# A two-layer hybrid trunk: mLSTM's causal mask by a selection on GpSimd, both chunks' decays in a step of their own, the gates' step first, and another order of the first loads

## The chip, the cores and the metric

One core of one Trainium2 chip runs the whole program. The metric is the device time of one execution in microseconds (us). A kernel's time is the median of its runs; lower is better.

## The reference, cut to what matters

Two layers over 1024 rows of 1024 features, all in float32. Each layer does this:

```
h = RMSNorm(x);  y = h @ W_in + b_in            # one projection for three groups
m_out = mLSTM(conv+SiLU(q), conv+SiLU(k), v, i, f)   # 4 heads x 64, chunkwise
h_out = HGRN2(...);  s_out = sliding window attention(...)
x = x + concat(m_out, h_out, s_out) @ W_out
x = x + relu(RMSNorm(x) @ W_up)^2 @ W_down      # 4096 wide
x = x + sigmoid(RMSNorm(x) @ W_g) * RMSNorm(p @ W_p)
```

The part that the change touches is the weight inside a chunk of mLSTM. With b the running sum of the log forget gates, i the input gates and m the stabiliser:

```
dmat    = where(causal, b_t - b_s + i_s, -inf)
w_intra = exp(dmat - m_t)                        # zero above the diagonal
s       = (q k^T) * w_intra
num     = s v + w_inter * (q C);   den likewise
```

So the weights of positions s later than t must come out as zero.

## The kernel before

**Dense work.** The rows are cut into two blocks of 512 (b = 0, 1). `gemm` works a product in slabs: one slab is two 128-row pieces of weights, loaded as `raw` on SyncE's queue, split into a rounded part `whi` (ScalarE, L395) and the remainder `wlo` (VectorE, L399), and used by 24 matmuls (4 output tiles x 2 pieces x 3 products) at L435 or L437. `gemm` yields after each slab. For layer 0 the `wlo` of block 0 is stored to memory by GpSimd's queue (L402) and loaded again for block 1 by the same queue (L397), into a ring of 4 buffers. In all VectorE splits 800 pieces.

**Mixers.** The three groups (`SWA`, `HGRN`, `MLSTM`) are generators of small steps, two of each for every (layer, block), one for each half block (hb) of 256 rows. `Emitter.run` emits one dense step, then as many mixer steps as a rate says, in turn among up to three active mixers. Counted with the last, empty one, `SWA` has 9 steps, `HGRN` 14 and `MLSTM` 9, so that a (layer, block) has 2 x 32 = 64. An `MLP` has 66 dense steps (2 of the norm, 8 x 4 of the up products, 16 x 2 of the down products). With `RATE_MLP` = 0.9 that makes 59 mixer steps; `PLE` goes on at 0.9. The mixers of block 1 of layer 0 are emitted in `MLP` and `PLE` of block 0 alone; those of layer 1 get 9 steps more in the projection before. Block 0 of layer 0 is mixed into the projection of block 1, at 2.5 steps to a slab. A scheduler then orders each engine's queue by emission, priority and what is ready; every engine works its queue in order.

**One MLSTM** (L1178 to L1302) covers two chunks of 128 rows. Its steps before the change: (1) convolution (L1192, L1194); (2) SiLU of q and k, copies into `qbd`, then the gates: transposes `pg` (L1209), the log sigmoid of 4 x 256 values (L354 to L357), two scans (L1217, L1218) and the rows `R` (a constant tile `G4`, L1220 to L1224) and their bfloat16 parts `Gb` (L1228 to L1231); (3) transposes `pt` of `R` (L1236), the decays between chunks (L1238), `cS`, `ee`, `dcy`; then for each chunk c two steps: (4, 6) the decays `pw` in a bank of PSUM, their exponentials `W` (L1259, 4 of 128x128), the scores `pS` (L1262) and the product `Pt` (L1265); (5, 7) the values and the state; (8) the output. The bank `pw` is begun by a matmul of an identity with a mask of 0 and -1e30 (L1253), on which four matmuls add the decays (L1255):

```
nc.tensor.matmul(pw3, self.identb, self.mmask.unsqueeze(1).broadcast_to([P, 4, P]), start=True, stop=False)
for h in range(4):
    nc.tensor.matmul(pw3[:, h, :], self.selb[:, h:h + 1].broadcast_to([P, P]), Gb[:, c * P:(c + 1) * P], start=False, stop=(h == 3))
```

The mixers, the norms' transposes (L498) and the transposes of `PLE` (L794) share 4 banks of PSUM (`mbank`).

**The opening.** `first_constants` emits WARM = 15 matmuls on a constant tile (L221) ahead of everything else. `load_x` asks for the first halves of 4 tiles of x, t = 0 and 2 on SyncE's queue, t = 1 and 3 on ScalarE's, and for the first two `raw` of the projection `skv` on SyncE's; then for the second halves. `first` interleaves the norm of block 0 (generator a) with the projection's slabs (generator c): a, c, c, a, then the rest of a (constants, mean square, its inverse root, transposes L574), then the rest of c.

Of the kernel before, what the change touches and what calls it, by code (L numbers as in the profile page):

```python
# [21 lines left out]
P = 128  # L22
# [16 lines left out]
RATE_IN00 = 1.9  # L39
RATE_IN01 = 2.5  # L40
RATE_IN = 0.7
RATE_MLP = 0.9
RATE_PLE = 0.9

ROOM = tuple(22 - 4 * max(0, (n + 2) // 4) + 2 for n in range(24)) + (8,)
# [111 lines left out]
class Trunk:  # L157
# [65 lines left out]
    def constants(self, rows):  # L223

        nc, io, cst = self.nc, self.io, self.cst
        L, S = self.L, self.S
        ap = nc.gpsimd
        nt = S // P
        ident = self.ident
        self.rs = [cst([P, 136], f"rows{l}") for l in range(L)]  # L230
        self.fb = cst([4, L], "fb")
        self.identb = cst([P, P], "identb", BF16)
        nc.vector.tensor_copy(self.identb, ident)
        mm = self.mmask = cst([P, P], "mmask", BF16)
        ap.memset(mm, 0.0)
        ap.affine_select(mm, mm, pattern=[[1, P]], compare_op=ALU.is_ge, fill=NEG, base=0, channel_multiplier=-1)
        am = self.amask = cst([P, 256], "amask", BF16)
        ap.memset(am, 0.0)
        ap.affine_select(am, am, pattern=[[1, 256]], compare_op=ALU.is_ge, fill=NEG, base=-1, channel_multiplier=-1)
        ap.affine_select(am, am, pattern=[[-1, 256]], compare_op=ALU.is_ge, fill=NEG, base=P, channel_multiplier=1)  # L240
        rm = self.rmask = cst([P, 512], "rmask", BF16)
        ap.memset(rm, 1.0)
        ap.memset(rm.rearrange("p (c t) -> p c t", t=P)[:, :, 0:1], 0.0)
        self.lmask = {}
        for w in (16, 8, 4, 2, 1):
            t = cst([P, 64], f"lm{w}", U8)
            ap.memset(t, 1)
            v = t.bitcast(I8)
            ap.affine_select(v, v, pattern=[[-2 * w, 64 // w], [0, w]], compare_op=ALU.is_ge, fill=0.0, base=0, channel_multiplier=1)
            ap.affine_select(v, v, pattern=[[2 * w, 64 // w], [0, w]], compare_op=ALU.is_ge, fill=0.0, base=w - 1, channel_multiplier=-1)  # L250
            self.lmask[w] = t
        self.selp = cst([P, 2, P], "selp")
        ap.memset(self.selp, 0.0)
        ap.memset(self.selp[64:68], 1.0)
        ap.affine_select(self.selp[64:68], self.selp[64:68], pattern=[[2, 2], [1, 2], [0, 64]], compare_op=ALU.is_equal, fill=0.0, base=0, channel_multiplier=-1)
        self.hind = cst([P, 2], "hind")
        ap.memset(self.hind, 0.0)
        ap.memset(self.hind[0:64, 0:1], 1.0)
        ap.memset(self.hind[64:128, 1:2], 1.0)

        self.qbd = cst([P, 2, 2, 256], "qbd")
        ap.memset(self.qbd, 0.0)
        self.hqb = []
        for i in range(2):
            t = cst([P, 2, 2, 2, 64], f"hqb{i}")
            ap.memset(t, 0.0)
            self.hqb.append(t)
        self.hqi = 0
        self.G4 = cst([P, 256], "G4")
        ap.memset(self.G4, 0.0)  # L270

        self.Gb = cst([P, 256], "Gb", BF16)
        ap.memset(self.Gb, 0.0)
        self.selb = cst([P, 4], "selb", BF16)
        ap.memset(self.selb, 0.0)
        for j in range(3):
            v = self.selb[32 * j:32 * j + 4]
            ap.memset(v, 1.0)
            end = ap.affine_select(v, v, pattern=[[-1, 4]], compare_op=ALU.is_equal, fill=0.0, base=0, channel_multiplier=1)
        with self.tc.issue_after(end.ins):  # L280
            for l in range(L):
                ap.dma_start(self.rs[l], io["rowS"][l:l + 1].broadcast_to([P, 136]))
            ap.dma_start(self.fb, io["fb"])
            rows(ap)
        self.cbd = cst([P, 2, 2, 65], "cbd")
        self.sbd = cst([P, 2, 2, 64], "sbd")
        self.ml = cst([4, 1], "ml")
        self.K = [[cst([P, 4, P], f"K{a}{b}", F32R) for b in range(2)] for a in range(2)]
        self.V = cst([P, 4, P], "V")
        self.kv_once = set()  # L290
# [229 lines left out]
    def load_x(self, b, src, first=False):  # L520
        X = [[None, None] for _ in range(4)]
        for h in range(2):
            for t in range(4):
                s = X[t][h] = self.get()
                eng = self.nc.gpsimd if not first else self.nc.scalar if (h, t % 2) == (0, 1) else self.nc.sync
                with self.tc.high_priority(2000) if first and h == 0 else nullcontext():
                    end = eng.dma_start(s[:, :512], src(b, t, h))
                    if first and h == 0 and t == 3:
                        self.x_asked = end
            if first and h == 0:  # L530
                self.early = [self.wraw(self.skv_rows(0, kp)) for kp in range(2)]
        return X

    def x_in(self, b, t, h):
# [643 lines left out]
    def MLSTM(self, l, b, hb, st):  # L1178
# [4 lines left out]
        if b == 0 and hb == 0:  # L1183
            nc.gpsimd.memset(self.cbd, 0.0)
            nc.gpsimd.memset(self.ml, 0.0)
        Y = [self.get() for _ in range(2)]
        a = self.get()
        for f in range(4):
            y = Y[f // 2][:, (f % 2) * 256:(f % 2) * 256 + 256]
            u = st["U"][f]  # L1190
            c0 = C_CW + 4 * f
            nc.scalar.activation(y, u[:, hb * 256:hb * 256 + 256], AF.Identity, scale=cols[:, c0:c0 + 1], bias=cols[:, C_CB + f:C_CB + f + 1])  # L1192
            for j in range(1, 4):
                nc.vector.scalar_tensor_tensor(y, u[:, hb * 256 + j:hb * 256 + j + 256], cols[:, c0 + j:c0 + j + 1], y, op0=ALU.mult, op1=ALU.add)  # L1194
        if hb == 1:
            self.put(*st["U"])
        yield
        Q, Kt = Y[0][:, :512], Y[1][:, :512]
        self.silu(Q, a[:, :512])
        self.silu(Kt, a[:, :512], 0.125)  # L1200
        Q3 = Q.rearrange("p (a t) -> p a t", a=2)
        K3 = Kt.rearrange("p (a t) -> p a t", a=2)
        for j in range(2):
            nc.vector.tensor_copy(self.qbd[j * 64:j * 64 + 64, :, j, :], Q3[j * 64:j * 64 + 64])

        pg = self.bank()
        for i in range(2):
# [23 lines left out]
        nc.vector.tensor_tensor(Gb[64:68], r1, Gb[32:36], op=ALU.subtract)  # L1231
        self.put(g, g2)
        yield
        pt = self.bank()
        for c in range(2):
            nc.tensor.transpose(pt[:, c * P:c * P + 100], R[0:100, c * P:(c + 1) * P], self.ident[0:100, 0:100])  # L1236
# [10 lines left out]
        ND = self.get()  # L1247
        kw = self.get()
        nd4 = ND[:, 0:520].rearrange("p (c h e) -> p c h e", c=2, e=65)
        for c in range(2):  # L1250
            pw = self.bank()
            pw3 = pw.rearrange("p (h t) -> p h t", t=P)
            nc.tensor.matmul(pw3, self.identb, self.mmask.unsqueeze(1).broadcast_to([P, 4, P]), start=True, stop=False)  # L1253
            for h in range(4):
                nc.tensor.matmul(pw3[:, h, :], self.selb[:, h:h + 1].broadcast_to([P, P]), Gb[:, c * P:(c + 1) * P], start=False, stop=(h == 3))  # L1255
            W = self.get()
            W3 = W[:, :512].rearrange("p (h t) -> p h t", t=P)
            for h in range(4):
                nc.scalar.activation(W3[:, h, :], pw3[:, h, :], AF.Exp, bias=cS[:, c, h:h + 1])  # L1259
            pS = self.bank()  # L1260
            for p in range(2):
                nc.tensor.matmul(pS[:, p * 256:p * 256 + 256].rearrange("p (h t) -> p h t", t=P), Kt[:, p * 256 + c * P:p * 256 + c * P + P],  # L1262
# [48 lines left out]
def trunk_kernel(ctx: ExitStack, tc: tile.TileContext, io, dims):  # L1311
# [29 lines left out]
    def first():  # L1341
# [4 lines left out]
        yield next(c)  # L1346
        yield next(a)
        k.behind = None
        yield from a
        yield from c  # L1350

# [65 lines left out]
```

## Time and profile before

| | |
|---|---|
| median of 3 runs | 2652.71 us (2652.69 to 2653.03) |
| profiled execution, its own time | 2653.13 us |
| its span, first to last instruction | 2651.4 us |
| TensorE matmuls, busy | 2636.1 us, 12719 instructions |
| VectorE busy | 1742.0 us |
| ScalarE busy | 1401.5 us |
| GpSimd busy | 106.1 us |
| granted TensorE clock, mean | 0.999 |

The span is what the trace sees; the profiled execution's own time is 1.7 us longer, and lies 0.4 us above the median of the runs. Busy time of matmuls is a union of rows that overlap each other, since a matmul starts before the one ahead of it has ended.

### The profile page before, as it was taken

The page shows a single profiled execution, that of the slowest core. Times are in us where ns is not written, and L with a number is a line of the kernel's source. Part 1 is how long each engine was busy: PE and PEld are TensorE (multiplying, and loading weights), DVE is VectorE, ACT ScalarE, POOL GpSimd, SP SyncE. Part 2 cuts the span into 40 slices and gives each one's busy share as a digit, 9 for nine tenths or more (in the row PEclk, how much of TensorE's full clock was granted, in tenths as well). Part 3 has the DMA queues.
Part 4 walks back from the last instruction along what each step waited for, and adds up shares of the span by engine and source line. Part 5 has one row for each costly group of instructions (what it writes and reads, how often), then busy time and mean ns, then how long its engine had stood idle before and what let it go on. Part 6 is the DMA issues. An engine that isn't in the chain of part 4 may idle for free.

```text
span 2651.4 us, 35073 instructions
## 1 busy us (share of the span) xinstructions
PE 2636.1 (99%) x12719; PEld 2143.3 (81%) x12719; DVE 1742.0 (66%) x3697; ACT 1401.5 (53%) x2924; POOL 106.1 (4%) x232
## 2 busy tenths in 40 slices
PE   9999999999999999999999999999999999999999
PEld 7877788887788888887788888888778888888887
DVE  5787757677678557776775755776677584443448
ACT  5456545455557544545654653554664464433336
POOL 3201100000000100000000010000000000000000
PEclk9999999999999999999999999999999999999999
DMA  7644532222222532222222253222222243332332
GB/s 220 199 115 121 144 110 80 88 80 80 84 84 90 151 100 80 88 87 73 80 88 96 97 155 93 77 88 80 78 82 88 96 135 104 96 96 95 104 104 80
DMA packets 138845, 270.54 MB, mean 102 GB/s; under 512 B 10672, under 2 KB 15920, under 8 KB 138672
## 3 DMA queue, kind: packets, MB, share of 16 engines
q1 hardware_dynamic: 119328, 224.03, 27.2%
q0 software_dynamic: 18480, 43.55, 5.5%
q8 instruction: 100, 1.64, 0.3%
q10 hardware_dynamic: 864, 0.72, 0.1%
q14 instruction: 73, 0.60, 0.1%
HBM read 249.39 MB, written 18.87 MB: 101 GB/s over the span
## 4 chain that ended last, share of the span: by engine, by line
PE 95%; DVE 2%; ACT 1%; issue 1%; DMA 1%; POOL 0%; POOLq 0%; ACTq 0%; DVEq 0%
PE gbank L437 52%; PE gbank L435 32%; PE mbank L498 1%; PE mbank L932 1%; PE mbank L999 1%; PE mbank L1142 1%; PE mbank L969 1%; PE gbank L467 1%; PE mbank L1262 1%; PE mbank L1269 1%; PE mbank L1158 0%; PE mbank L1127 0%; PE mbank L945 0%; PE mbank L1272 0%; ACT junk L476 0%
## 5 line engine op out<-in xcount | busy, mean ns | idle before, releaser
L437 PE MATMUL gbank<-whi,slot 128*128 128x512 f32 (+1 forms) x4160 | 1303.2, 391 | 0.0
L395 ACT ACTIVATE whi<-raw 128x512 fp32r<-128x512 f32 (+1 forms) x836 | 515.2, 621 | 830.7 <-PE gbank L437 492.1
L437 PEld LDWEIGHTS gbank<-whi,slot 128*128 128x128 f32 x4160 | 772.1, 188 | 170.4 <-issue 2.8
L399 DVE TENSOR_TENSOR wlo<-raw,whi 128x512 fp32r<-128x512 f32 (+1 forms) x800 | 538.3, 679 | 545.2 <-ACT whi L395 542.2
L435 PE MATMUL gbank<-slot,whi 128*128 128x512 f32 x2560 | 824.7, 397 | 0.0
L437 PE MATMUL gbank<-wlo,slot 128*128 128x512 f32 (+1 forms) x2080 | 807.9, 389 | 0.4 <-DVE wlo L399 0.3
L435 PEld LDWEIGHTS gbank<-slot,whi 128*128 128x128 f32 x2560 | 480.3, 188 | 110.7 <-issue 3.3
L435 PE MATMUL gbank<-slot,wlo 128*128 128x512 f32 x1280 | 505.9, 395 | 0.5 <-DMA wlo<-lo 0.4
L437 PEld LDWEIGHTS gbank<-wlo,slot 128*128 128x128 f32 x2080 | 391.5, 188 | 81.2 <-DVE wlo L399 0.8
L435 PEld LDWEIGHTS gbank<-slot,wlo 128*128 128x128 f32 x1280 | 241.1, 188 | 52.3 <-DMA wlo<-lo 1.3
L759 DVE SCALAR_TENSOR_TENSOR slot<-gbank,nrs,slot 128x512 f32<-128x512 f32 x256 | 191.4, 748 | 48.7 <-PE gbank L437 45.6
L367 DVE TENSOR_TENSOR slot<-slot 128x512 fp32r<-128x512 f32 x144 | 99.1, 690 | 86.9 <-ACT slot L366 86.1
L370 DVE SCALAR_TENSOR_TENSOR slot<-mbank,cols,slot 128x512 fp32r<-128x512 f32 x112 | 78.8, 744 | 20.3 <-ACT slot L369 20.0
L745 ACT ACTIVATE slot<-gbank 128x512 f32<-128x512 f32 x128 | 74.9, 585 | 32.4 <-PE gbank L435 32.3
L366 ACT ACTIVATE slot<-slot 128x512 fp32r<-128x512 f32 x144 | 89.6, 629 | 2.6
L369 ACT ACTIVATE slot<-mbank,cols 128x512 fp32r<-128x512 f32 x112 | 72.3, 686 | 20.7 <-PE mbank L498 14.8
L746 ACT ACTIVATE slot<-slot 128x512 f32<-128x512 f32 x128 | 80.6, 629 | 2.5
L476 ACT ACTIVATE junk<-slot 128x512 bf16<-128x512 f32 x96 | 60.1, 626 | 34.3 <-DVE slot L759 16.9
L979 ACT ACTIVATE slot<-slot,snm 128x256 f32<-128x256 f32 (+1 forms) x128 | 61.8, 484 | 29.2 <-DVE snm L976 29.2
L788 POOL DMA_DIRECT2D slot<-in_p_dram x8 | 5.7, 719 | 1412.1 <-PE gbank L437 469.8
L498 PE MATMUL mbank<-ident,slot 128*128 128x128 f32 x384 | 60.7, 273 | 0.5 <-ACT slot L1259 0.5
L1096 ACT ACTIVATE slot<-slot 128x256 f32<-128x256 f32 x56 | 23.5, 420 | 71.3 <-DVE slot L1095 71.1
(274 smaller groups left out, 2287.3 us busy)
## 6 DMA issues: line engine op xcount, KB each, us to landing
raw<-in_w_up_dram SPq DMA_DIRECT2D x128, 512.0 KB, 3.6
raw<-in_w_down_dram SPq DMA_DIRECT2D x128, 512.0 KB, 3.5
raw<-in_w_in_dram SPq DMA_DIRECT2D x80, 512.0 KB, 3.8
raw<-in_w_ple_gate_dram SPq DMA_DIRECT2D x32, 512.0 KB, 3.5
lo<-wlo POOLq DMA_DIRECT2D x40, 256.0 KB, 4.3
wlo<-lo POOLq DMA_DIRECT2D x40, 256.0 KB, 3.0
raw<-in_w_out_dram SPq DMA_DIRECT2D x16, 512.0 KB, 4.4
raw<-in_w_out_dram SPq DMA_DIRECT2D x32, 256.0 KB, 4.3
```

Of the source, the lines that this page charges most:

```text
L366: first = nc.scalar.activation(r_(hi), src, AF.Copy)
L367: nc.vector.tensor_tensor(r_(lo), src, hi, op=ALU.subtract)
L369: first = nc.scalar.activation(r_(hi), src, AF.Copy, scale=scale)
L370: nc.vector.scalar_tensor_tensor(r_(lo), src, scale, hi, op0=ALU.mult, op1=ALU.subtract)
L395: nc.scalar.activation(hi[:, :n], raw[:, kk, :n], AF.Copy)
L399: nc.vector.tensor_tensor(lo[:, :n], raw[:, kk, :n], hi.bitcast(F32)[:, :n], op=ALU.subtract)
L435: nc.tensor.matmul(banks[i], wa[:, sl], ta, start=first, stop=last)
L437: self.last_mm = nc.tensor.matmul(banks[i][:, :n], ta, wa[:, :n], start=first, stop=last)
L498: nc.tensor.transpose(ps[:, t * P:(t + 1) * P], X[t][h][:, k4 * P:(k4 + 1) * P], self.ident)
L745: nc.scalar.activation(u[:, :512], ps, AF.Relu)
L746: nc.scalar.activation(u[:, :512], u[:, :512], AF.Square)
L759: nc.vector.scalar_tensor_tensor(x, ps, r2[:, i:i + 1], x, op0=ALU.mult, op1=ALU.add)
```

## The change

The mask matmul, its identity and its mask tile go. The four matmuls of the decays each begin their own quarter of the bank. Behind the exponentials GpSimd writes zero where s is later than t (`affine_select` on the 128 x 512 tile `W`, one for each chunk, 16 in the program). Both chunks' decays, exponentials and selections become one step, ahead of the two chunks' scores and values. The gates become the first step, the convolution the second, SiLU with the copies the third: `MLSTM` has 11 steps in place of 9, a (layer, block) 68 in place of 64, and `RATE_MLP` goes from 0.9 to 1.0. The moved blocks of `MLSTM` are not changed inside, and are left out of the diff below. In the opening the two early `raw` loads are asked for behind x's t = 2, and one slab more of `skv` is emitted ahead of the rest of the norm.

```diff
-RATE_MLP = 0.9
+RATE_MLP = 1.0
...
-        self.identb = cst([P, P], "identb", BF16)
-        nc.vector.tensor_copy(self.identb, ident)
-        mm = self.mmask = cst([P, P], "mmask", BF16)
-        ap.memset(mm, 0.0)
-        ap.affine_select(mm, mm, pattern=[[1, P]], compare_op=ALU.is_ge, fill=NEG, base=0, channel_multiplier=-1)
...
+                    if first and h == 0 and t == 2:
+                        self.x_sp = end
             if first and h == 0:
-                self.early = [self.wraw(self.skv_rows(0, kp)) for kp in range(2)]
+                with self.tc.issue_after(self.x_sp.ins):
+                    self.early = [self.wraw(self.skv_rows(0, kp)) for kp in range(2)]
...
+        Ws = []
         for c in range(2):
             pw = self.bank()
-            nc.tensor.matmul(pw3, self.identb, self.mmask.unsqueeze(1).broadcast_to([P, 4, P]), start=True, stop=False)
             for h in range(4):
-                nc.tensor.matmul(pw3[:, h, :], self.selb[:, h:h + 1].broadcast_to([P, P]), Gb[:, c * P:(c + 1) * P], start=False, stop=(h == 3))
+                nc.tensor.matmul(pw3[:, h, :], self.selb[:, h:h + 1].broadcast_to([P, P]), Gb[:, c * P:(c + 1) * P], start=True, stop=True)
             W = self.get()
             for h in range(4):
                 nc.scalar.activation(W3[:, h, :], pw3[:, h, :], AF.Exp, bias=cS[:, c, h:h + 1])
+            nc.gpsimd.affine_select(W3, W3, pattern=[[0, 4], [1, P]], compare_op=ALU.is_ge, fill=0.0, base=0, channel_multiplier=-1)
+            Ws.append((W, W3))
+        yield
+        for c in range(2):
+            W, W3 = Ws[c]
             pS = self.bank()
...
         k.behind = None
+        yield next(c)
         yield from a
         yield from c
```

## Rows read from the trace of the kernel before

**Rows 1.** The page: engines' busy time, and the chain that ended last.

```profile
PE 2636.1 (99%) x12719; PEld 2143.3 (81%) x12719; DVE 1742.0 (66%) x3697; ACT 1401.5 (53%) x2924; POOL 106.1 (4%) x232
PE 95%; DVE 2%; ACT 1%; issue 1%; DMA 1%; POOL 0%; POOLq 0%; ACTq 0%; DVEq 0%
```

**Rows 2.** Waits of PE: who for whom, total us, times, longest.

```profile
PE mbank L1236 <- DVE G L1222: 2.8, 3, 1.0
...
PE mbank L498 <- ACT slot L1259: 0.5, 1, 0.5
```

**Rows 3.** Groups by line: busy us, mean ns | idle before.

```profile
L437 PE MATMUL gbank<-whi,slot 128*128 128x512 f32 (+1 forms) x4160 | 1303.2, 391 | 0.0
L1253 PE MATMUL mbank<-mmask,identb 128*128 128x512 bf16 x16 | 6.2, 387 | 0.0
L1259 ACT ACTIVATE slot<-mbank,cS 128x128 f32<-128x128 f32 x64 | 19.3, 364 | 9.0 <-PE mbank L1255 8.9
L1265 DVE TENSOR_TENSOR slot<-mbank,slot 128x512 f32<-128x512 f32 x16 | 11.0, 688 | 5.3 <-ACT slot L1259 5.2
```

**Rows 4.** The chain in order of time, one dense stretch: start, us, what.

```profile
337.05 35.28 PE gbank L437 x152
```

**Rows 5.** Timeline of a first chunk, 734 to 738 us: start, us, engine.

```profile
735.68 0.39 PE L1253 MATMUL mbank<-mmask,identb 128*128 128x512 bf16 x1
735.90 0.39 PE L1255 MATMUL mbank<-Gb,selb 128*128 128x128 bf16 x4
736.13 1.08 PE L1262 MATMUL mbank<-qbd,slot 128*128 128x256 f32 x4
...
736.86 0.58 PE L435 MATMUL gbank<-slot,whi 128*128 128x512 f32 x1
...
737.28 0.39 PE L435 MATMUL gbank<-slot,wlo 128*128 128x512 f32 x1
```

**Rows 6.** Timeline of a gates' step, 789 to 796 us.

```profile
789.20 0.40 ACT L354 ACTIVATE slot<-slot 4x256 f32<-4x256 f32 x1
...
793.73 0.27 DVE L1223 TENSOR_SCALAR G<-G,slot 4x128 f32<-4x128 f32 x1
793.92 0.27 PEld L1236 LDWEIGHTS mbank<-ident,G 100*128 100x128 f32 x2 [1.25 <-PE gbank L437]
793.96 0.41 PE L1236 MATMUL mbank<-ident,G 100*128 100x100 f32 x2 [0.84 <-DVE G L1222]
```

**Rows 7.** Timeline at the end of the first MLP, 799 to 805 us.

```profile
802.51 0.62 ACT L1259 ACTIVATE slot<-mbank,cS 128x128 f32<-128x128 f32 x2
...
803.18 0.66 PE L498 MATMUL mbank<-ident,slot 128*128 128x128 f32 x4 [0.55 <-ACT slot L1259]
```

**Rows 8.** Groups of POOL by line.

```profile
L397 POOL DMA_DIRECT2D wlo<-lo x40 | 21.4, 534 | 156.3 <-PE gbank L437 70.9 <-PE gbank L435 54.7 <-DVE rt L347 27.6
...
L239 POOL TENSOR_SCALAR_AFFINE_SELECT amask<-amask 128x256 bf16<-128x256 bf16 x1 | 0.4, 399 | 0.0
...
L214 POOL TENSOR_SCALAR_AFFINE_SELECT ident<-ident 128x128 f32<-128x128 f32 x1 | 0.3, 287 | 0.1
```

**Rows 9.** Timeline of the opening, 0 to 60 us.

```profile
1.25 0.42 SPq L377 DMA_DIRECT2D raw<-in_w_skv_dram  x1
...
1.72 0.46 SPq L527 DMA_DIRECT2D slot<-in_x_dram  x1
...
6.77 1.89 PEld L498 LDWEIGHTS mbank<-ident,slot 128*128 128x128 f32 x16
6.99 1.91 PE L498 MATMUL mbank<-ident,slot 128*128 128x128 f32 x16
...
8.38 0.73 ACT L393 ACTIVATE whi<-raw 128x264 fp32r<-128x264 f32 x2
```

**Rows 10.** DMA issues from 1.7 to 1.73 us: last column us to landing.

```profile
slot<-in_x_dram SPq DMA_DIRECT2D x1, 256.0 KB, 4.8
```

**Rows 11.** Busy time by stretch: PE, PEld, DVE, ACT, POOL, clock, DMA, GB/s.

```profile
14.00:25.00 11.00, 10.34 (x82) 9.85 (x81) 7.89 (x19) 9.49 (x26) 3.69 (x8) 1.00 0.87 257
```

More of the change, by code (lines that the diff above doesn't have):

```diff
@@ L1185, in MLSTM @@
             nc.gpsimd.memset(self.ml, 0.0)
[L1186 to L1204, printed above, removed]
         pg = self.bank()
@@ L1233, in MLSTM @@
         yield
+        Y = [self.get() for _ in range(2)]
+        a = self.get()
+        for f in range(4):
+            y = Y[f // 2][:, (f % 2) * 256:(f % 2) * 256 + 256]
+            u = st["U"][f]
+            c0 = C_CW + 4 * f
+            nc.scalar.activation(y, u[:, hb * 256:hb * 256 + 256], AF.Identity, scale=cols[:, c0:c0 + 1], bias=cols[:, C_CB + f:C_CB + f + 1])
+            for j in range(1, 4):
+                nc.vector.scalar_tensor_tensor(y, u[:, hb * 256 + j:hb * 256 + j + 256], cols[:, c0 + j:c0 + j + 1], y, op0=ALU.mult, op1=ALU.add)
+        if hb == 1:
+            self.put(*st["U"])
+        yield
+        Q, Kt = Y[0][:, :512], Y[1][:, :512]
+        self.silu(Q, a[:, :512])
+        self.silu(Kt, a[:, :512], 0.125)
+        Q3 = Q.rearrange("p (a t) -> p a t", a=2)
+        K3 = Kt.rearrange("p (a t) -> p a t", a=2)
+        for j in range(2):
+            nc.vector.tensor_copy(self.qbd[j * 64:j * 64 + 64, :, j, :], Q3[j * 64:j * 64 + 64])
+        yield
         pt = self.bank()
@@ L1259, in MLSTM @@
                 nc.scalar.activation(W3[:, h, :], pw3[:, h, :], AF.Exp, bias=cS[:, c, h:h + 1])
+            nc.gpsimd.affine_select(W3, W3, pattern=[[0, 4], [1, P]], compare_op=ALU.is_ge, fill=0.0, base=0, channel_multiplier=-1)
+            Ws.append((W, W3))
+        yield
+        for c in range(2):
+            W, W3 = Ws[c]
             pS = self.bank()
```

## The prediction

> **What bounds the kernel now.** I read the page's busy times and its chain first: PE's matmuls cover 2636.1 of 2651.4 us, and PE holds 95% of the chain that ended last [rows 1]. So a change is worth the PE time that it takes out and the PE waits that it ends; work on the other engines counts only where PE comes to wait for it. Second, the waits of PE: they are few, and the longest entry is L1236, the transposes of the gates' rows, behind VectorE (2.8 us in 3 waits) [rows 2]. The reader is to see there that mLSTM's gates are the largest single thing PE waited for. Third, the groups by line, for what one instruction costs [rows 3]; and the chain in order of time, for what one costs in a stream: 152 dense matmuls in 35.28 us are 0.232 us each [rows 4], where the groups say 0.391 [rows 3]. The rows of matmuls overlap, so PE time is counted from start to start. A slab of 24 is 24 x 0.232 = 5.57 us; that is the cover that a mixer step has in `MLP`.
>
> **The change, part by part.**
>
> *The mask matmul goes.* From the start of L1253 to the start of L1255 are 735.90 - 735.68 = 0.22 us [rows 5]. There are 16 [rows 3], so PE loses 16 x 0.22 = 3.5 us of work. Bounds: nothing, if whatever follows it is late anyway; 16 x 0.387 = 6.2 us by the busy mean [rows 3]. PE is full, so I take 3.5. The four matmuls of the decays are the same in number and size. The removed constants lay on GpSimd and VectorE ahead of any use, under the opening's matmuls: nothing.
>
> Here the Trainium skill has a rule, Perfetto Trace Analysis, section Identifying the Most-Contended Engine: matmul busy time misjudges TensorE because matmuls are pipelined. By that rule the sum below goes with 3.5; by the busy mean it would be 2.7 us further down, 2643.0. The trace agrees with the rule: 0.232 against 0.391 for the same instruction [rows 3, 4].
>
> *The gates come two steps earlier.* Before, one step holds SiLU and the gates, and the next one holds L1236. The timeline shows the chain: ScalarE begins the gates' absolute value at 789.20, VectorE ends the last row of `R` at 793.73 + 0.27 = 794.00, and PE has already stood for 0.84 us [rows 6]. That is 4.8 us for the gates, hardly less than a slab's 5.57, with SiLU's instructions ahead of them on the same engines. After the change two steps (convolution, SiLU) lie between the gates and L1236, that is two slabs or more in `MLP` and about 4.5 us in the projection at 2.5 steps to a slab (5.57 / 2.5 = 2.2 us a step). What was waited for is long done. The waits of L1236 are 2.8 us [rows 2]; and since a dense matmul's row reaches 0.391 - 0.232 = 0.16 us beyond the point where the next could start [rows 3, 4], each of the 3 waits costs 0.16 more than it shows: 3.3. I take 3.0, bounds 0 (another wait takes its place) and 3.5. What is late next: `pS` needs `qbd` and SiLU's results; it comes three steps behind them, as far as before. The banks are no later.
>
> *The end of the first MLP.* 66 dense steps at 0.9 gave 59 mixer steps, so of the 64 of block 1 in layer 0 five lay in `PLE`; at 1.0 it is 66 of 68, so two. The decays of the second half block then no longer lie between `PLE`'s transposes, where L498 waited 0.55 us for a bank that L1259 held [rows 7]. I take 0.5 off; bounds 0 and 0.6. All other mixers end inside their `MLP` at either rate: (1, 0) and (1, 1) have 9 steps from the projection, and 59 remain for 66.
>
> *Both chunks' decays in one step.* One more place in PE's queue where dense work is interrupted, in each of 8 `MLSTM`. A row that shows such a place: behind the scores, the second dense matmul starts 737.28 - 736.86 = 0.42 us after the first instead of 0.23 [rows 5]. Taken whole, 8 x 0.19 = 1.5 us lost. That tail belongs to the scores' own 256-column matmuls, which have run longer than their starts tell; the decays are short, so I take 0 and keep 1.5 for the range. Two banks of 4 are held for 8 exponentials of 0.364 = 2.9 us [rows 3] where one was held for 1.5; a norm's transposes beside it could wait as in rows 7, 0.55 us at most times the one place of that kind that stays.
>
> *The selection on GpSimd.* No row has a 128x512 one. The nearest: 0.287 us for 128x128 in float32 and 0.399 for 128x256 in bfloat16 [rows 8]. By the slope, 0.399 + 2 x (0.399 - 0.287) = 0.62; as four of the small ones, 4 x 0.287 = 1.15. I take 0.7, both ends kept. 16 of them are 11 us (10 to 18) on an engine that is busy for 106 of 2651 [rows 1]. What hides them: in `MLP` the product L1265 of the first chunk comes one mixer step, a slab of 5.57 us, behind the decays, and needs 4 x 0.364 + 0.7 = 2.2 us (at most 2.6); the second chunk's comes another slab later. So PE pays nothing. If the cover is gone, VectorE stands in L1265, and behind it the splits L399 of the next slab. In the projection, at 2.2 us a step, the first chunk's product can be late by up to 0.4 us in two places; VectorE already waits there (5.3 us in all before L1265 [rows 3]) and PE hardly felt it. On GpSimd's queue the loads of `wlo` stand behind the selection in that stretch; 4 selections lie there, and each can hold a load for its own length and for the exponentials. A load waits for PE to free its buffer anyhow [rows 8]. Taken 0, bound 4 x 1.15 = 4.6 us lost.
>
> *The opening.* x's t = 2 is asked for at 1.72 and lands 4.8 us later, at 6.5 [rows 9, 10]; the transposes that need it load their weights at 6.77, right behind the 15 warming matmuls [rows 9]. So x was not what PE waited for, and 0.47 us earlier (1.72 - 1.25) buys nothing. The first `raw` is asked for 0.47 us later; its first reader starts at 8.38 [rows 9], so it loses nothing either. The slab of `skv` that moves ahead: in 14 to 25 us PE is idle for 11.00 - 10.34 = 0.66 us in all [rows 11], which bounds a gain, and I take the same for a loss; value 0.
>
> *Sum.* 3.5 + 3.0 + 0.5 = 7.0 us off. The profiled execution's own time of 2653.1 becomes 2646.1; the median lies 0.4 lower, so 2652.7 - 7.0 = **2645.7 us**.
>
> **The rivals.**
>
> *A, only the matmuls go.* The new order of steps makes as much PE waiting as it ends: another mixer's transposes stand where L1236 stood. For it: all positions in the queues shift with 68 steps for 64, and PE's other waits were of that kind too. Against it: no chain in the new `MLSTM` is as long as the gates' with only one step behind it. 2652.7 - 3.5 = 2649.2.
>
> *B, more goes.* The remaining waits of the mixers shrink as well, since `MLSTM`'s steps are shorter and VectorE's queue is smoother; or the mask matmul's start-to-start undervalues it, as in the busy mean. 2652.7 - 6.2 - 3.5 - 0.6 - 1.0 = 2641.4.
>
> *C, slower: the product L1265 stands behind the selection.* Place: VectorE's queue, with the weight splits behind L1265. If every selection passes on its whole upper length to PE, the loss is 16 x 1.15 = 18.4, and the time 2652.7 - 7.0 + 18.4 = 2664.1. From 7.0 / 16 = 0.44 us a product on, the gain is eaten; from (7.0 + 5.3) / 16 = 0.77 it is slower by 0.2%. Against it: the cover of 5.57 us counted above. The Trainium skill speaks for it, GPSIMD Engine Reference, section Key points: GpSimd shares its SBUF interfaces with VectorE and contends with instructions that have two SBUF inputs, as the splits have; by that rule a selection also slows a split beside it, at most by its own length, which is C's price. No row here shows a large selection beside a split.
>
> *D, no change:* the mask matmuls were hidden behind something else. The chain [rows 1] speaks against it.
>
> **How the numbers follow.** A 0.2% step is 5.3 us, about what can be told from no change, so the borders are 2647.4 and 2658.0. My forecast 0.52, A 0.25, B 0.12, C 0.08, D 0.03. The forecast's own spread is the bounds of the opening (0.7), the interruptions (1.5) and the gates (3.5 for 3.0): 2644.5 to 2648, and about a tenth of it lies above 2647.4. Faster: 0.47 + 0.12 = 0.59; slower, the part of C beyond 0.77 us a product, 0.05; the same 0.36. For 8 in 10 the range reaches down to B's time, 2641, and up beyond A to A with half the bound of the `wlo` loads, 2649.2 + 2.3 = 2651.5; what is left out is D, most of C and what lies below B.
>
> **What the changed profile would show.** Right: no row of L1253's kind; no wait of the `pt` transposes on `G` above 0.3 us; selections of 0.6 to 1.2 us on POOL, 16 of them; PE's busy time down by about what the span loses less 3 us; the first transposes of the opening still at 6.8 to 7.0. Wrong: PE waiting for `wlo` of L399 behind L1265, or for `wlo` from memory in the stretch of 150 to 320 us, or for a bank that the exponentials hold; selections far above 1.2 us. The prediction fails low if PE's waits in the other mixers shrink too, and high if the new order makes new ones.

## The result, and the profile after it

The changed kernel takes 2666.84 us (median, 2666.16 to 2670.22), against 2652.70 for the kernel before beside it: 14.1 us slower, ratio 1.0056 (95% interval 1.004 to 1.0072). The prediction said 2645.7 and faster.

In the line numbers after the change the matmuls of the dense work are L430 and L432, the splits L390 (`whi`) and L394 (`wlo`), the relu L743, the gates' rows L1199 to L1203, the convolution L1219 and L1221, SiLU and the log sigmoid L349 to L352, `pt` L1235, the decays L1254, the selection L1260 and the product `Pt` L1270.

The page of the kernel after, busy times and chain, answers to [rows 1]:

```profile
PE 2641.0 (99%) x12703; PEld 2141.7 (80%) x12703; DVE 1739.9 (65%) x3696; ACT 1396.8 (52%) x2924; POOL 117.7 (4%) x246
PE 91%; DVE 5%; ACT 2%; issue 1%; DMA 0%; ACTq 0%; DVEq 0%
```

PE has 16 matmuls fewer and is busy 4.9 us longer, in a span of 2664.4 us, 13.0 longer. So idle time grew by 8.1 and busy time by 4.9 (2.5 of it are the slower matmuls shown below). VectorE's share of the chain went from 2% to 5% with the same busy time: nothing was added to VectorE, it is waited for at another place. Which place, the waits of PE after the change say; they answer to [rows 2]:

```profile
PE gbank L432 <- DVE wlo L394: 3.9, 2, 3.0
PE gbank L432 <- ACT slot L743: 2.9, 2, 1.5
PE gbank L430 <- DVE wlo L394: 2.0, 3, 0.7
...
PE mbank L1235 <- DVE G L1202: 1.0, 1, 1.0
...
PE mbank L1235 <- DVE G L1203: 0.9, 1, 0.9
```

The gates' transposes are no longer first; two waits on them are left, both in the projection of block 1. In their place stand the dense matmuls, waiting for a `wlo` that VectorE splits too late (5.9 us) and for a relu that ScalarE does too late (2.9 us). Before, PE's waits for a late split were this one, and it lies in the opening, at 17.89 us:

```profile
PE gbank L437 <- DVE wlo L399: 0.3, 1, 0.3
```

Two of the three waits for the gates in the kernel before lay in that projection too (PE's timeline of before; the third is the one of [rows 6]):

```profile
267.88 0.41 PE L1236 MATMUL mbank<-ident,G 100*128 100x100 f32 x2 [0.91 <-DVE G L1222]
299.50 0.28 PE L1236 MATMUL mbank<-ident,G 100*128 100x100 f32 x1 [1.00 <-DVE G L1222]
```

So there the move ended neither of them: the two after it are as long.

The longest one, in the first `MLP`, by engine. VectorE's timeline of the kernel after:

```profile
757.66 0.68 DVE L1196 TENSOR_TENSOR_SCAN slot<-rmask,slot 4x256 f32<-4x256 bf16 x1
...
762.88 0.48 DVE L1221 SCALAR_TENSOR_TENSOR slot<-slot,cols 128x256 f32<-128x256 f32 x1
...
765.15 0.42 DVE L1210 TENSOR_TENSOR Gb<-slot,Gb 4x256 bf16<-4x256 f32 x1
...
766.26 0.87 DVE L1221 SCALAR_TENSOR_TENSOR slot<-slot,cols 128x256 f32<-128x256 f32 x2
...
767.72 3.25 DVE L1221 SCALAR_TENSOR_TENSOR slot<-slot,cols 128x256 f32<-128x256 f32 x8
770.88 0.69 DVE L394 TENSOR_TENSOR wlo<-raw,whi 128x512 fp32r<-128x512 f32 x1
771.48 0.48 DVE L1221 SCALAR_TENSOR_TENSOR slot<-slot,cols 128x256 f32<-128x256 f32 x1
```

ScalarE's, and PE's:

```profile
765.75 1.38 ACT L390 ACTIVATE whi<-raw 128x512 fp32r<-128x512 f32 x2 [4.00 <-PE gbank L432]
769.41 0.63 ACT L349 ACTIVATE slot<-slot 128x512 f32<-128x512 f32 x1 [2.28 <-DVE slot L1221]
```

```profile
762.45 0.50 PE L432 MATMUL gbank<-wlo,slot 128*128 128x512 f32 x1 [0.87 <-DVE wlo L394]
...
768.20 0.40 PE L1254 MATMUL mbank<-Gb,selb 128*128 128x128 bf16 x4
771.62 0.80 PE L432 MATMUL gbank<-wlo,slot 128*128 128x512 f32 x1 [3.02 <-DVE wlo L394]
772.21 1.06 PE L432 MATMUL gbank<-whi,slot 128*128 128x512 f32 x2
773.06 0.63 PE L432 MATMUL gbank<-wlo,slot 128*128 128x512 f32 x1
773.49 0.63 PE L432 MATMUL gbank<-whi,slot 128*128 128x512 f32 x1
...
777.13 0.39 PE L432 MATMUL gbank<-wlo,slot 128*128 128x512 f32 x1
```

The reader is to see that both halves of `whi` were done at 767.13 (765.75 + 1.38), and that the split of the first began at 770.88, because eight of the convolution's twelve VectorE instructions stood ahead of it. Three more, and the gates' rows, fill the stretch before; the twelfth comes behind the split. In the kernel before, the twelve of the same half block lay between 764.65 and 780.28 us with the splits among them, and the gates came after, from 789 on [rows 6]. VectorE's timeline of the kernel before:

```profile
764.65 0.48 DVE L1194 SCALAR_TENSOR_TENSOR slot<-slot,cols 128x256 f32<-128x256 f32 x1
...
767.97 1.27 DVE L1194 SCALAR_TENSOR_TENSOR slot<-slot,cols 128x256 f32<-128x256 f32 x3
...
770.44 0.69 DVE L399 TENSOR_TENSOR wlo<-raw,whi 128x512 fp32r<-128x512 f32 x1
...
779.28 1.00 DVE L1194 SCALAR_TENSOR_TENSOR slot<-slot,cols 128x256 f32<-128x256 f32 x2
```

The relu comes late in the same manner, one engine further. In the next `MLP` with mixers, ScalarE's and then PE's timeline of the kernel after:

```profile
1379.85 0.63 ACT L349 ACTIVATE slot<-slot 128x512 f32<-128x512 f32 x1 [1.74 <-DVE slot L1221]
1380.39 0.58 ACT L743 ACTIVATE slot<-gbank 128x512 f32<-128x512 f32 x1
```

```profile
1381.02 0.50 PE L432 MATMUL gbank<-whi,slot 128*128 128x512 f32 x1 [1.47 <-ACT slot L743]
```

SiLU's first instruction stands in ScalarE's queue until the convolution of q, its input, is done (1.74 us), the relu behind it, and PE waits 1.47 us for the relu.

These are not two chance places. Each `MLP` with mixers holds two half blocks of `MLSTM`, six in all, and in the kernel after every wait of a dense matmul for a split or a relu lies in or beside the stretch of one of their convolutions: 696.46 (0.67 us), 762.45 and 771.62, 1310.65 (0.69), 1381.02, 1970.92 (0.67) and 2041.34 (1.44).

There is a second thing in PE's rows at 771.62. Behind the wait the dense matmuls start 0.43 us apart (773.06, 773.49) and not 0.23 [rows 4]. The windows of the same stretch (columns as in [rows 11]; the third figure from the end is the granted clock) say why:

```profile
766.00:768.60 2.60, 2.60 (x20) 1.88 (x18) 2.60 (x7) 1.02 (x2) 0.00 (x0) 1.00 0.00 0
768.60:771.60 3.00, 0.00 (x0) 0.00 (x0) 3.00 (x8) 1.89 (x3) 0.00 (x0) 0.74 0.00 0
771.60:774.00 2.40, 2.38 (x6) 1.92 (x7) 2.40 (x5) 0.63 (x1) 0.00 (x0) 0.50 0.14 37
774.00:776.90 2.90, 2.90 (x9) 2.26 (x7) 1.85 (x5) 1.35 (x4) 0.00 (x0) 0.50 0.72 221
776.90:780.00 3.10, 3.10 (x15) 2.54 (x14) 1.09 (x2) 1.76 (x4) 0.00 (x0) 1.00 0.27 103
```

TensorE's granted clock fell during the idle 3.00 us and was 0.50 (1.2 GHz) for the 5.3 us behind it, then 1.00 (2.4 GHz) again. Thirteen dense matmuls from 771.62 to 777.13 took 5.51 us in place of 13 x 0.232 = 3.02, so the clock cost 2.5 us on top of the wait's 3.0. The Trainium skill (TensorE: Matmul & The Clock Gate, section Part 1: The HAM clock gate) says that the clock halves when the engine has been idle and returns with activity; the trace agrees, 0.50 behind this wait.

### The profile page after: what moved, and what is told of

The parts are those of the page before. It is cut to its first block, busy times and chain, and to the rows that moved or that the text cites. A ratio compares the mean times of both kernels' runs of the same rounds, so it can differ in the third digit from the quotient of the medians.

```text
span 2664.4 us, 35039 instructions
## 1 busy us (share of the span) xinstructions
PE 2641.0 (99%) x12703; PEld 2141.7 (80%) x12703; DVE 1739.9 (65%) x3696; ACT 1396.8 (52%) x2924; POOL 117.7 (4%) x246
## 4 chain that ended last, share of the span: by engine, by line
PE 91%; DVE 5%; ACT 2%; issue 1%; DMA 0%; ACTq 0%; DVEq 0%
PE gbank L432 50%; PE gbank L430 30%; PE mbank L930 1%; PE mbank L493 1%; PE mbank L997 1%; PE mbank L967 1%; PE mbank L1140 1%; DVE slot L1221 1%; PE gbank L462 1%; DVE wlo L394 1%; PE mbank L1156 0%; PE mbank L1267 0%; ACT whi L390 0%; PE mbank L1274 0%; DVE slot L1147 0%
## 5 line engine op out<-in xcount | busy, mean ns | idle before, releaser
L432 PE MATMUL gbank<-whi,slot 128*128 128x512 f32 (+1 forms) x4160 | 1303.5, 391 | 3.0 <-ACT slot L743 2.9
L390 ACT ACTIVATE whi<-raw 128x512 fp32r<-128x512 f32 (+1 forms) x836 | 515.0, 622 | 871.3 <-PE gbank L432 537.5
L432 PEld LDWEIGHTS gbank<-whi,slot 128*128 128x128 f32 x4160 | 772.3, 188 | 176.0 <-ACT slot L743 4.7
L394 DVE TENSOR_TENSOR wlo<-raw,whi 128x512 fp32r<-128x512 f32 (+1 forms) x800 | 538.0, 679 | 554.4 <-ACT whi L390 551.5
L430 PE MATMUL gbank<-slot,whi 128*128 128x512 f32 x2560 | 825.9, 397 | 0.3 <-DVE slot L592 0.3
L432 PE MATMUL gbank<-wlo,slot 128*128 128x512 f32 (+1 forms) x2080 | 808.6, 390 | 4.2 <-DVE wlo L394 3.9
L430 PEld LDWEIGHTS gbank<-slot,whi 128*128 128x128 f32 x2560 | 479.9, 188 | 107.0 <-issue 1.0
L430 PE MATMUL gbank<-slot,wlo 128*128 128x512 f32 x1280 | 505.7, 395 | 2.1 <-DVE wlo L394 2.0
L432 PEld LDWEIGHTS gbank<-wlo,slot 128*128 128x128 f32 x2080 | 391.6, 188 | 91.4 <-DVE wlo L394 5.6
L430 PEld LDWEIGHTS gbank<-slot,wlo 128*128 128x128 f32 x1280 | 240.6, 188 | 55.1 <-DVE wlo L394 4.7
L743 ACT ACTIVATE slot<-gbank 128x512 f32<-128x512 f32 x128 | 74.9, 585 | 19.3 <-PE gbank L430 19.2
L1260 POOL TENSOR_SCALAR_AFFINE_SELECT slot<-slot 128x512 f32<-128x512 f32 x16 | 11.6, 726 | 1139.3 <-ACT slot L1258 1005.9
```

Of the source, the lines that this page charges most:

```text
L390: nc.scalar.activation(hi[:, :n], raw[:, kk, :n], AF.Copy)
L394: nc.vector.tensor_tensor(lo[:, :n], raw[:, kk, :n], hi.bitcast(F32)[:, :n], op=ALU.subtract)
L430: nc.tensor.matmul(banks[i], wa[:, sl], ta, start=first, stop=last)
L432: self.last_mm = nc.tensor.matmul(banks[i][:, :n], ta, wa[:, :n], start=first, stop=last)
L743: nc.scalar.activation(u[:, :512], ps, AF.Relu)
```

## The experiments

Each was timed beside the kernel before on its own chip (2652.6 to 2652.9). The expectations name theories by number. **1**: gates and convolution, now in adjacent steps with nothing between them, fill one stretch of VectorE's queue, so that the splits come late, and SiLU, waiting for the convolution, holds ScalarE. **2**: the decays' own step or the selection. **3**: the rate and the number of steps. **4**: the scheduler takes the convolution early wherever it stands. **5**: the order of PE's small matmuls; in the last two runs 5 and 6 are new, and stated there. Several times came out above the range that the theory they speak for had been given; this is said with each.

**One part at a time.** The opening's edits alone:

```diff
+                with self.tc.issue_after(self.x_sp.ins):
+                    self.early = ...
+        yield next(c)
```

> The kernel before with the opening's edits alone (x's t = 2 ahead of the two early weight loads, one slab of skv ahead of the rest of the norm). Theory 1, gates: nothing here, 2652.7 within 1.5. Theory 2, decays and selection: the same. Theory 3, the mixers' rate and step count: the same. If this alone costs more than 3 us, the opening is part of the loss and none of the three is whole.

2653.46 us, ratio 1.0003 (0.9994 to 1.0013). No effect. The selection alone, both chunks' steps as before:

```diff
-            nc.tensor.matmul(pw3, self.identb, self.mmask..., start=True, stop=False)
+            nc.gpsimd.affine_select(W3, W3, pattern=[[0, 4], [1, P]], ...)
```

> The kernel before with the mask by a selection alone, in its place between a chunk's exponentials and its product; steps, order and rate as before. Theory 1: PE loses the mask matmuls, 2652.7 - 3.5 = 2649.2 (2647 to 2651). Theory 2: the product waits behind the selection and the splits behind the product: 2656 or more. Theory 3: as theory 1.

2649.51 us, 0.9988 (0.9978 to 0.9997): 3.1 us off. It is the fastest of all that ran, and beats both kernels. The rate alone:

```diff
-RATE_MLP = 0.9
+RATE_MLP = 1.0
```

> The kernel before with RATE_MLP 1.0 alone. Theory 1 (the gates' and the convolution's VectorE work in one stretch holds the weight splits): 2652.7 within 2. Theory 3 (denser mixer steps): 2657 or more.

2655.89 us, 1.0011 (1.0002 to 1.002): 3.1 us lost, more than theory 1 allowed and less than theory 3 asked. The gates as a step of their own ahead of the convolution, SiLU a step, rate 1.0, mask matmul kept:

```diff
+        (gates)
+        yield
         (convolution)
         yield
         (SiLU, copies)
-        (gates)
         yield
```

> The kernel before with the gates as the first step, SiLU in a step behind the convolution and RATE_MLP 1.0; mask matmul, decays by chunk and opening as before. Theory 1: the loss of the change sits here, because the gates' and the convolution's VectorE work now lies in one stretch and the transposes and decays run ahead of SiLU, with ScalarE standing in SiLU's first instruction and the dense evacuations and splits behind it: 2664 to 2670. Theory 2: the loss sits in the decays' own step with the selection, so this one gains the waits of the gates' transposes: 2649 to 2652. Theory 3 (rate): 2660 or more.

2664.58 us, 1.0045 (1.003 to 1.006): 12.0 us lost, 8.9 of them beyond the rate. The changed kernel with the gates put back behind SiLU, all else as changed:

```diff
-        (gates)
-        yield
         (convolution)
         yield
         (SiLU, copies)
+        (gates)
         yield
```

> The changed kernel with the gates put back behind SiLU (convolution; SiLU and gates; transposes; both chunks' decays with selections; then the chunks), RATE_MLP 1.0 and the opening of the change kept. Theory 1: the loss is gone, 2646 to 2651. Theory 2: the loss stays, 2660 or more. Theory 3: the loss stays, since the rate is 1.0: 2658 or more.

2652.34 us, 0.9999 (0.999 to 1.0009). So the loss needs the gates in front; selection, own step, opening and rate together come out at nothing, 1.3 us above theory 1's range. PE waits for no split there, and from here to the kernel as changed are 14.5 us.

**Is it the meeting with the convolution?** Gates first as above, and two empty steps (`yield`) between the gates and the convolution:

```diff
         (gates)
         yield
+        yield
+        yield
         (convolution)
```

> The kernel with the gates first (as the earlier run with the gates alone, 2664.6) and two empty steps between the gates and the convolution, so that the two lie two slabs further apart in the order of emission; RATE_MLP 1.0. Theory 1: most of the 12 us comes back, 2653 to 2657. Theory 3 (more steps at this rate cost by themselves): no better than 2664. Theory 4 (the scheduler takes the convolution early whatever its step, so only the amount of work matters): 2660 to 2666.

2658.48 us, 1.0022 (1.0012 to 1.0031): 6.1 of the 12.0 come back, between the ranges of theories 1 and 4. Gates first as above, with 4 of the convolution's 12 VectorE instructions left in each half block (two of three taps are left out of the computation), and the kernel before with the same cut as its control:

```diff
-            for j in range(1, 4):
+            for j in range(1, 2):
```

> The kernel with the gates first, and of the convolution's three VectorE taps for each feature tile only one (4 instructions in place of 12; the convolution's other two taps are left out). Theories 1 and 4: the loss comes from 26 VectorE instructions of gates and convolution ahead of the splits, so cutting 8 of them takes most of it: 2654 to 2657. Theory 3: the loss stays, 2662 or more. A theory 5, that the order of PE's small matmuls costs by itself: the loss stays too.

> Control to the run before: the kernel before with the same two taps of the convolution left out. All theories: VectorE is not what PE waits for there, 2652.7 within 1.5.

2659.35 us, 1.0024 (1.0015 to 1.0034), and 2653.44 us, 1.0002 (0.9992 to 1.0011). The same VectorE work taken out is worth 5.2 us behind the gates (theory 1 had asked for 7.6 or more) and nothing in the kernel before. The gap alone could be doubted, since empty steps also move every later step against the slabs; the cut moves none. Theory 1 stands for 5 to 6 of the 9 us. Gates first alone has such places too. In its trace PE waits once in each of the six half blocks of the `MLP`s, for a split or a relu, 0.64 to 1.39 us and 5.9 in all, each time while that half block's convolution is on VectorE; with the rate alone it waits in none. The first of the six, on ScalarE, VectorE and PE (there `whi` is L395, the split L399 and the convolution L1222; `whi` was ready at 692.60):

```profile
691.27 1.33 ACT L395 ACTIVATE whi<-raw 128x512 fp32r<-128x512 f32 x2 [0.98 <-PE gbank L435]
694.86 2.86 DVE L1222 SCALAR_TENSOR_TENSOR slot<-slot,cols 128x256 f32<-128x256 f32 x7
697.64 0.68 DVE L399 TENSOR_TENSOR wlo<-raw,whi 128x512 fp32r<-128x512 f32 x1
698.38 0.50 PE L435 MATMUL gbank<-slot,wlo 128*128 128x512 f32 x1 [0.67 <-DVE wlo L399]
```

With the gap no wait for a split is left in any `MLP`, with the cut one of 0.8 us; waits for the relu stay in both, 2.3 us in four and 2.6 us in three.

**Is it the rate?** Gates first at 0.9, and the changed kernel at 0.9:

> The gates first as in the run with the gates alone (2664.6), but with RATE_MLP left at 0.9. If the rate's 3.1 us and the gates' 9 us add up: 2661.5 (2660 to 2663). If the pile-up of gates and convolution needs the denser rate: 2653 to 2657. If the gates cost the same at either rate and the rate's own price is another thing: 2664.

> The changed kernel with RATE_MLP 0.9 alone put back. Adding up: 2666.8 - 3.1 = 2663.7 (2661 to 2665). If the rate is what makes the late splits: 2655 or less.

2664.62 us, 1.0045 (1.0029 to 1.0062), and 2664.48 us, 1.0045 (1.003 to 1.006). In gates first the rate's 3.1 us don't come off: against the kernel before it is 11.9 us slower at 0.9 and 12.0 at 1.0, so that 8.9 is the price of the move at rate 1.0 only. In the changed kernel 2.4 us come off, though its longest wait grows to 4.9 us. By stages, in gates first alone at 0.9, the first `MLP` and the `PLE` behind it together stand at +3.1 us against the kernel before (+1.0 at rate 1.0), since, as I take it, the added steps spill into `PLE`; the other two `MLP`s with mixers give the 2.5 us back.

**The decays' own step, at 0.9.** The kernel before with the selection and the own step; and the same with the gates as a step between convolution and SiLU:

```diff
+            Ws.append((W, W3))
+        yield
+        for c in range(2):
+            W, W3 = Ws[c]
```

> The kernel before with the selection and with both chunks' decays in a step of their own; order of the gates, rate and opening as before. From the four parts timed so far (selection -3.1, rate +3.1, opening +0.8, all of them with the own step -0.3) the step itself would be -1.1: 2648.5 (2647 to 2650). Rival, the decays' step costs and something else paid for it: 2651 or more.

> As the run before (selection, decays in a step of their own, rate 0.9, old opening), with the gates as a step between the convolution and SiLU: behind the convolution they don't share its stretch, and SiLU's step then lies between them and their transposes. If the waits of the gates' transposes (about 3 us) can be had without the pile-up: 2645 to 2647. If gates ahead of SiLU pile up with SiLU as they did with the convolution: 2650 or more.

2657.00 us, 1.0016 (1.0007 to 1.0025), and 2656.61 us, 1.0015 (1.0005 to 1.0024). Both are 8 us or more above what was expected; against the selection alone the own step costs 7.5 us at this rate (2657.0 - 2649.5). The timeline of the first of these shows what happened as `PLE` begins, and its windows the clock there:

```profile
801.72 0.40 PE L1231 MATMUL mbank<-ident,G 100*128 100x100 f32 x1 [3.72 <-DVE G L1217]
```

```profile
800.00:804.00 4.00, 2.28 (x12) 2.31 (x13) 3.46 (x12) 0.03 (x1) 0.17 (x1) 0.69 0.01 2
804.00:808.00 4.00, 4.00 (x19) 3.63 (x18) 2.80 (x5) 2.62 (x6) 0.00 (x0) 0.50 0.00 0
808.00:812.00 4.00, 4.00 (x27) 3.41 (x27) 3.17 (x5) 2.78 (x5) 0.00 (x0) 0.96 0.43 135
```

The gates' transposes, spilt into `PLE` with hardly any dense work to cover them, waited 3.72 us, and the clock was at 0.50 behind it. The other one has a wait of 4.01 us there, of a dense matmul for a copy on VectorE, and a clock of 0.54 and 0.60 in the two stretches of 4 us around and behind it. In windows of 3 us from the start to 2640 us the granted clock is under 1.00 in four kernels of this study: the changed kernel (longest wait of PE 3.0 us), these two (3.7 and 4.0), and the changed kernel at 0.9 (4.9). In all others, where the longest wait is 1.8 us or less, it is 1.00 in each window.

**The decays' own step beside gates first.** The changed kernel with the decays back in two steps for each chunk; and with two empty steps between gates and convolution (rate 1.1, so that 72 steps fit):

```diff
-            Ws.append((W, W3))
-        yield
-        for c in range(2):
-            W, W3 = Ws[c]
```

```diff
-RATE_MLP = 1.0
+RATE_MLP = 1.1
...
         (gates)
         yield
+        yield
+        yield
         (convolution)
```

> The changed kernel with the decays, scores and values back in two steps for each chunk: gates first, selection, opening, rate 1.0. Theory 1 (the pile-up of gates and convolution is the whole loss, and the decays' own step only adds to it where they meet): the loss of gates first alone less the selection's gain, 2664.6 - 3.1 = 2661.5, range 2659 to 2664, with the 3.0 us wait for wlo in the first MLP gone. Theory 2 (the decays' own step has no part): as changed, 2666.8. Theory 2b (the own step is the larger part): below 2657.

> The changed kernel with two empty steps between the gates and the convolution, rate 1.1 so that the 72 steps still fit the MLP. Theory 1: the convolution's 12 VectorE instructions leave the gates' stretch, so at least the 6 us that the same gap gave back without the other edits come back, and the extra of the changed kernel too: 2655 to 2661. Theory 2 (the decays' own step sets the loss): nothing comes back, 2665 to 2668.

2660.70 us, 1.003 (1.0018 to 1.0042), and 2658.44 us, 1.0023 (1.0013 to 1.0033). So the own step is worth 6.1 us beside gates first (2666.8 - 2660.7), though at this rate it cost nothing without it. The last two runs ask whether that is its standing price, or one wait that happens to fall there: the changed kernel with `RATE_MLP` at 1.05 and at 1.1, which moves the steps against the slabs and nothing else.

```diff
-RATE_MLP = 1.0
+RATE_MLP = 1.05
```

> The changed kernel at RATE_MLP 1.05. Theory 5 (the extra 6 us are one long wait and the half clock behind it): where the trace shows no wait of PE of 3 us or more and the granted clock stays at 1.00, 2659 to 2662; where it shows one with 0.50 behind it, 2664 to 2668. Theory 6 (the decays' own step costs beside gates first wherever it falls): 2665 to 2668 at full clock too.

> The changed kernel at RATE_MLP 1.1, without the empty steps of the kernel that had 2658.4 at this rate. Theory 5: 2660 to 2664 at full clock, some 5 us more if one wait of 3 us or more is there with half the clock behind it. Theory 6: 2666 to 2669 at full clock. If it is at 2658 to 2660, the rate and not the empty steps gave that kernel its 8 us.

2660.80 us, 1.003 (1.0019 to 1.0042), and 2664.85 us, 1.0046 (1.0031 to 1.0061), both at full clock up to 2640 us. At 1.05 the 6 us are gone with the own step in place, 5.1 of them in the first `MLP` and `PLE` (table below), where the one long wait and its clock had been: theory 5 holds there. The time at 1.1 lies above theory 5's range and below theory 6's: 4 us more than at 1.05 without any long wait, +4.5 in each of the other two `MLP`s. Where the steps fall against the slabs is worth that much by itself. At 1.1 without the empty steps 6.4 us more are lost than with them, so the empty steps and not the rate gave the kernel with the gap its time. The waits of PE at 1.05 and then at 1.1 show theory 1's waits, shorter and more of them:

```profile
PE gbank L430 <- DVE wlo L394: 4.5, 5, 1.1
PE gbank L432 <- DVE wlo L394: 1.6, 1, 1.6
```

```profile
PE gbank L430 <- DVE wlo L394: 3.2, 3, 1.1
PE gbank L432 <- DVE wlo L394: 3.1, 3, 1.1
```

**Can the gates gain at all?** The changed kernel with the gates as a step between convolution and SiLU, rate 1.0; and the kernel before with the selection, the gates there too, rate 1.0 (the order of the steps against that of the kernel before):

```diff
         (convolution)
         yield
+        (gates)
+        yield
         (SiLU, copies)
-        (gates)
         yield
```

> The changed kernel with the gates as a step between the convolution and SiLU in place of first. Theory 1: nothing ready runs ahead into the gates' stretch, the transposes have one step of cover, no late splits: as the changed kernel with the gates behind SiLU (2652.3) less the waits of the transposes that it still had (2 to 3 us), 2649 to 2652. Theory 4 (any place ahead of SiLU puts gates and convolution side by side): 2657 to 2665.

> The kernel before with the selection in place, the gates as a step between the convolution and SiLU, and the rate at 1.0; decays, scores and values as before. Theory 1: the selection's 3.1 and up to 3 of the transposes' waits against up to 3.1 for the rate: 2648 to 2652. Theory 4: 2656 to 2662.

2653.15 us, 1.0003 (0.9993 to 1.0012), and 2653.23 us, 1.0001 (0.9991 to 1.001). No pile-up of the size of gates first, so theory 4 falls; but no gain either, both times are above theory 1's ranges. The waits of PE with the gates behind SiLU (2652.34 us), and with the gates in between (2653.15), the others of the changed kernel's edits in both:

```profile
PE mbank L1234 <- DVE G L1222: 2.1, 3, 0.8
PE mbank L1234 <- DVE G L1220: 1.9, 2, 1.0
```

```profile
PE gbank L432 <- DVE wlo L394: 1.6, 2, 0.8
...
PE mbank L1235 <- DVE G L1212: 1.3, 2, 1.1
...
PE gbank L432 <- ACT whi L388: 0.6, 1, 0.6
PE gbank L432 <- ACT slot L743: 0.6, 1, 0.6
```

The transposes' waits go from 4.0 to 1.3 us, as the prediction wanted; 2.8 us of waits for `wlo`, `whi` and the relu come instead.

**Where the time lies.** Counted from the traces by the starts of the dense matmuls of each stage, us against the kernel before (first `MLP` and `PLE` together, since steps spill from one to the other; the projection of block 1; the other two `MLP`s with mixers):

```
                    IN(0,1)  MLP+PLE(0,0)  MLP(0,1)  MLP(1,0)
rate alone           -0.7       -1.3         +1.2      +2.0
gates behind SiLU    -0.9       -1.9         +0.6      +0.5
gates between        -1.5       -2.0         +0.7      +1.5
gates first alone    +1.0       +1.0         +3.7      +4.0
changed, no own step +0.1       -0.0         +2.7      +3.2
changed              -0.1       +5.2         +3.1      +3.6
changed, rate 1.05   -0.1       +0.1         +2.3      +2.4
changed, rate 1.1    -0.2       +0.5         +4.5      +4.5
```

Each row is one execution. The rate doesn't reach the projection, so the -0.7 of the rate alone there is their spread. Against the rate alone, gates first costs some 2 us in each `MLP` with mixers and 1.7 in the projection; the changed kernel's extra is in the first `MLP` alone, where the wait of 3.02 us stands.

## Why the prediction was wrong, by its steps

The 14.1 us by parts, each the difference of two runs against the kernel before: rate +3.1; gates first +8.9 (12.0 - 3.1); selection and opening -4.2 (7.8 for the changed kernel without the own step, less 12.0); own step +6.3 (14.1 - 7.8). The parts hold in this order only: at rate 0.9 gates first costs 11.9, and taken last, out of the changed kernel, 14.5 (2666.84 - 2652.34).

*The mask matmul* was right: 3.5 predicted from start to start, 3.1 measured. The busy mean's 6.2 was not.

*The gates two steps earlier* is the step that failed. "What was waited for is long done" was true in the `MLP`s, where no wait of `pt` is left. It was not in the projection, where two of the three waits lay: by the prediction's own numbers the cover there is 4.5 us for a chain of 4.8, and the waits stayed (0.91 and 1.00 before, 1.0 and 0.9 after). But under "what is late next" I followed only the mLSTM's own chain, to `pS` and `qbd`. I didn't ask what VectorE and ScalarE would do in the stretch to which the gates moved. The chain of 4.8 us that I had read from [rows 6] went ahead of the convolution's 12 instructions of 0.48 us, which wait for nothing that the gates make. The splits L394 have priority in emission, but their input is made late in a slab, and the instructions that were ready stood in the queue ahead of them. So a wait of small transposes became a wait of the dense stream. The term was -3.0 with the bounds -3.5 and 0; it measured +8.9. Of this 5 to 6 us are shown to be the meeting with the convolution (the cut with its control, and the gap); some 3 are left. With the gap and with the cut the relu's waits, 2.3 and 2.6 us, are PE's largest; that they are the 3 is argued only, since no run takes SiLU out of that stretch. A bound of 0 for an edit that moves a chain of 4.8 us on ScalarE and VectorE was wrong in itself: a wait that takes the place of another can be larger.

*The end of the first MLP* was right where I looked (no wait of the norm's transposes on the exponentials is left; 0.5 predicted, at most 0.6, and 1.3 found in the first `MLP` and `PLE`, with a spread of 0.7 in one execution), and had no term for the rest: the same rate packs the steps closer in the two `MLP`s that had room, +1.2 and +2.0 us. The rate alone is +3.1. What it is there that costs PE time stays open: the sum of PE's waits is the same (9.5 against 9.3 us) and its busy time 2.5 us longer.

*Both chunks' decays in one step* at 0, bound +1.5: right at rate 1.0 without gates first (2652.3 against a sum of rate and selection of 2652.7), and beside it when the rate is 1.05 (2660.8 against 2660.7 for two steps at 1.0); at 0.9 it cost 7.5, more than half of it in the first `MLP` and the `PLE` into which the steps spill. In the kernel as changed it came to +6.3: its steps put the convolution where the split waits 3.0 us, and the clock adds 2.5, together 5.5 of it. I had no term for the clock. It stood at 0.999 in the profile and no row that I had read shows it low, so nothing there gave its price; that a long wait could cost nearly twice its length should have been a rival.

*The selection* was right. The groups of the kernel after:

```profile
L1260 POOL TENSOR_SCALAR_AFFINE_SELECT slot<-slot 128x512 f32<-128x512 f32 x16 | 11.6, 726 | 1139.3 <-ACT slot L1258 1005.9 <-DVE wlo L394 127.6 <-issue 5.2
L1270 DVE TENSOR_TENSOR slot<-mbank,slot 128x512 f32<-128x512 f32 x16 | 11.0, 687 | 2.0 <-PE mbank L1267 1.8
```

0.726 us where I took 0.7; and VectorE's idle time ahead of the product fell from 5.3 us [rows 3] to 2.0, none of it for the selection. So rival C, the slower one that I had priced, falls, though its sign came out. Its price, a split slowed by the length of a selection, isn't there: the seven splits that ran beside a selection took 0.68 to 0.75 us, against 0.69 in the median of all. Of the selections eleven took 0.63 to 0.65 us and five 0.89 to 1.00; three of the five had begun while a split ran. *The opening* was right at 0 (+0.8 with an interval across 0): the first transposes start 0.29 us earlier than in [rows 9], and nothing follows.

```profile
6.70 1.91 PE L493 MATMUL mbank<-ident,slot 128*128 128x128 f32 x16
```

Rival A had the mechanism, another wait in the place of the one removed, and held it to be a draw. Of the signs that I named for a wrong prediction, PE waiting for `wlo` was one, but behind L1265, not behind the convolution.

## What to carry to other kernels

When a step is moved off one wait, read the queue of each engine that it uses in the stretch where it arrives, and name the instructions of the critical stream that will stand behind it; two blocks of work that wait for nothing of each other and both lie ahead of a weight split are to be kept apart (two empty steps between them gave back 6.1 of 12.0 us here). Price one long wait of TensorE with the slower matmuls behind it, and look at the granted clock behind each wait of several us. A change of several edits is worth timing in parts: here one edit alone, the selection, gives 3.1 us, and the others take it back.

## What was not expected of the hardware

One idle stretch of TensorE of 3.0 us in the middle of a program took its clock down and left it at 0.50 for the 5.3 us behind it, at a price of 2.5 us (the windows above); in the kernels whose longest wait was 1.8 us or less no window up to 2640 us shows it low. A short wait costs more than it shows as well: behind one of 0.87 us at 762.45 in the kernel after, the next dense matmul starts 0.34 us later and not 0.23, and the same 0.34 stands behind the waits of 1.47 us at 1381.02 and, in gates first alone, of 0.67 us at 698.38.
